# First layer of a two-layer trunk: gate values normalised on ScalarE, the gating half of the projection issued ahead of the convolution's LayerNorm, 13 convolution taps on ScalarE and GpSimd

## The chip, the cores and the metric

The kernel runs on one core of one Trainium2 chip. The time is device microseconds of one execution. The core's engines are named as in the profile: PE is the matmul engine (TensorE), with PEld for its weight loads; DVE is VectorE; ACT is ScalarE; POOL is GpSimd; SP issues the DMAs. Every engine works through its own instructions in a fixed order and waits on semaphores for the others.

## The reference

The trunk has two layers, each followed by an MLP, with 1024 tokens of width 1024, all float32. Only the first layer's mixer is touched by the change:

```python
def conv_gmlp_mixer(h, w_in, conv_w, conv_b, conv_ln_g, conv_ln_b,
                    sg_ln_g, sg_ln_b, sg_w, sg_b, w_out):
    z = h @ w_in
    a_val = z[..., :CONV_CH]                 # 512 channels each
    a_gate = z[..., CONV_CH:2 * CONV_CH]
    z_sg = z[..., 2 * CONV_CH:]
    a = a_val * jax.nn.sigmoid(a_gate)
    a = depthwise_conv(a, conv_w, width=31) + conv_b
    a = jax.nn.silu(layernorm(a, conv_ln_g, conv_ln_b))
    zs = jax.nn.gelu(z_sg, approximate=False)
    u = zs[..., :SG_CH]
    v = layernorm(zs[..., SG_CH:], sg_ln_g, sg_ln_b)
    v = v.reshape(B, S // 128, 128, SG_HEADS, SG_HEAD_DIM)
    v = jnp.einsum('gpq,bnqgc->bnpgc', sg_w, v) + sg_b.T[None, None, :, :, None]
    sg = u * v.reshape(B, S, SG_CH)
    return jnp.concatenate([a, sg], axis=-1) @ w_out

# per layer
shift, scale, gate = jnp.split(c_act @ mod_w + mod_b, 3, axis=-1)
h = rmsnorm(x, g) * (1 + scale) + shift
x = x + gate * mixer(h)
```

Here `depthwise_conv` stands for the reference's centred convolution along the tokens with one 31-tap filter per channel. The MLP that follows has its own `shift`, `scale` and `gate`.

## The kernel before, in words

Activations lie with channels on the 128 partitions and tokens along the free axis, in two column halves `c` of 512 tokens (`C = 512`, `NC = 2`). Every matmul product is made of three float32r matmuls (`mm3`, L128 to L132: high by high, high by low, low by high); so each weight stripe of 128x1024 is loaded as `raw`, cast to its high part `whi` on ACT (L112) and subtracted to its low part `wlo` on DVE (L113), in `prep`. Activations are split in the same way (`split`, L258: `zh` on ACT L259, `zl` on DVE L260).

The program is written in the order of the computation, but a planner of the framework (a timeline simulation at build time) sets each engine's fixed order from its own costs; `tc.high_priority` and manual dependencies bend it. The order on the chip is therefore that of the built program, not of the code.

The first layer goes through these stages:

1. RMSNorm of both column halves. `Norm.add` (L222) squares a block on ACT and adds it on DVE to a running sum; `Norm.fin` (L235) sums over partitions with one matmul against ones, and `rstd_of` makes the reciprocal root. The first 16 conditioning vectors are made by `mods(k)` beside this. Each is one `mod_unit` (L142): a DMA of 512 KB into `mraw`, and a DVE multiply with reduction (L147).
2. The projection of the convolution's values and gates; `glu` (L434) writes the padded inputs `ap` of four channel blocks of 128.
3. The gate values `vg`: projection, Gelu on ACT, statistics on DVE (L497, L498), and for each of 8 token chunks the normalisation as a DVE tensor_scalar (L509).
4. The projection of `u`, Gelu, and `gating(g)` for four heads: four small matmuls (L527), the eviction `tt` (L530) and the product (L534) on DVE, for each `g` and `c`. Then the split into `z[4..7]`.
5. The convolution (L579 to L603). For each of four blocks `i`, ACT makes the product of one tap (`pr`), POOL adds it to `a1` (L596): 11 taps in all, 10 of them with an add. DVE does the other `DVE_TAPS = 20` as a chain in PSUM, `ca` (L598 and L600), and adds `a1` at the end (L601).
6. LayerNorm over the 512 convolution channels: sums by PE with ones (L612), `y - mean` on DVE (L616), the squares on ACT, `rstd_of`; then, per block and column half, `y*rstd`, the sigmoid on ACT with the affine in its scale and bias, the affine itself on DVE (L633), the product on DVE (L635), and the split into `z[0..3]`.
7. The output projection in two halves (`project_half`): half 1 reads the gating's `z[4..7]`, half 0 the convolution's `z[0..3]`. Each is 16 outputs of 12 matmuls, each output followed by a residual update on DVE (`upd`, L283), which needs the conditioning's gate vectors: `queue_mod(0, [16])` queues these eight units, and `bg(n)` issues n queued units. 24 further units (`queue_mod(1, ...)`) are for the MLP. The planner orders each of these background units behind a chosen matmul (`newest`, L132) or behind POOL's last tap add (`conv_end`), and all of them share two buffers:

```python
            raw = cond.tile([P, D], F32, name="mraw", tag="mraw", bufs=2)
```

8. The MLP (first line in the trace: `mm3` with `b` or the first layer's `h`), unchanged, as is the whole second layer.

Half 1 of the projection stands in the code behind the LayerNorm, and so do all background units:

```python
        queue_mod(0, [16])
        bg(100)
        queue_mod(1, [8, 0], conv_end)
        queue_mod(1, [16])
        bg(18)
```

## Time and profile before

| what | us |
|---|---|
| median of 3 runs (lowest, highest) | 2315.51 (2313.82, 2316.77) |
| profiled execution: its own time | 2312.99 |
| profiled execution: span | 2311.2 |
| PE busy (share of the span) | 2188.4 (95%) |
| DVE busy | 1867.0 (81%) |
| ACT busy | 1180.8 (51%) |
| POOL busy | 238.5 (10%) |
| granted TensorE clock, mean | 0.982 |

The span runs from the first to the last instruction; the time has 1.8 us more around it. Busy times of different engines overlap, so only the waits of the engine that is nearly always busy, PE, add up to time. In the slices, one digit stands for 57.8 us, in tenths. In rows of instructions, the name left of the arrow is written, those right of it are read, and the bracket is the idle time ahead of it on its engine with what ended it.

### The profile page before, as it was taken

The numbers are of one execution on the slowest core, as the hardware profiler recorded it, in microseconds if no ns is written. First come the engines' busy times: TensorE is split into PE (matmuls) and PEld (weight loads), VectorE is DVE, ScalarE is ACT, GpSimd is POOL, SyncE is SP. The second block draws the span as 40 slices with busy tenths as digits, with TensorE's granted clock in tenths as the row PEclk, the third lists the DMA queues.
The fourth block names the chain that finished last, engine by engine and source line by source line (L and its number), as shares of the span: only waits on it lengthen the run. The fifth ranks groups of instructions, "written<-read, shape, count | busy, mean of one in ns | idle before, by whom it ended". The sixth has DMA issues, their size and how long they took to land. (4 is left out here: it accounts for less than half of the span.)

```text
span 2311.2 us, 27508 instructions
## 1 busy us (share of the span) xinstructions
PE 2188.4 (95%) x10144; PEld 1800.3 (78%) x10144; DVE 1867.0 (81%) x2582; ACT 1180.8 (51%) x1753; POOL 238.5 (10%) x126
## 2 busy tenths in 40 slices
PE   4997599999999999979999999999999999999997
PEld 3786387778888888858888888887778888888886
DVE  8899899997785976986878878876699659578497
ACT  4554246643534535455666666654366354353455
POOL 0484000000000000031111111111100000000002
PEclk9998799999999999989999999999999999999999
DMA  8221553838448267233445333361353461643712
GB/s 319 84 73 46 192 168 131 319 112 284 178 165 284 97 224 250 91 114 90 93 92 109 68 90 73 77 205 51 114 216 121 163 229 48 214 140 111 245 45 73
DMA packets 113863, 335.17 MB, mean 145 GB/s; under 512 B 20576, under 2 KB 23520, under 8 KB 112704
## 3 DMA queue, kind: packets, MB, share of 16 engines
q1 hardware_dynamic: 113728, 333.41, 44.6%
q8 instruction: 80, 1.31, 0.2%
q14 instruction: 55, 0.45, 0.1%
HBM read 279.79 MB, written 53.58 MB: 144 GB/s over the span
## 5 line engine op out<-in xcount | busy, mean ns | idle before, releaser
L131 PE MATMUL ps<-b,whi 128*128 128x512 f32 (+1 forms) x1808 | 701.4, 389 | 6.7 <-DVE b L260 6.7
L130 PE MATMUL ps<-b,whi 128*128 128x512 f32 (+1 forms) x1808 | 692.8, 390 | 5.1 <-ACT b L259 4.6
L132 PE MATMUL ps<-b,wlo 128*128 128x512 f32 (+1 forms) x1808 | 693.6, 388 | 1.9 <-DVE wlo L260 1.9
L259 ACT CAST whi<-raw 128x1024 fp32r<-128x1024 f32 (+1 forms) x225 | 236.5, 1051 | 356.1 <-PE ps L131 310.1
L131 PEld LDWEIGHTS ps<-b,whi 128*128 128x128 f32 x1808 | 340.7, 188 | 79.7 <-DVE b L260 9.5
L130 PEld LDWEIGHTS ps<-b,whi 128*128 128x128 f32 x1808 | 340.3, 188 | 77.0 <-ACT b L259 3.9
L132 PEld LDWEIGHTS ps<-b,wlo 128*128 128x128 f32 x1808 | 340.4, 188 | 72.1 <-DVE wlo L260 2.7
L260 DVE TENSOR_TENSOR wlo<-raw,whi 128x1024 fp32r<-128x1024 f32 x224 | 273.0, 1219 | 137.4 <-ACT whi L259 135.5
L130 PE MATMUL ps<-hh,whi 128*128 128x512 f32 x576 | 225.0, 403 | 40.7 <-ACT hh L254 23.5
L131 PE MATMUL ps<-hl,whi 128*128 128x512 f32 x576 | 229.4, 399 | 4.1 <-DVE hl L255 2.6
L132 PE MATMUL ps<-hh,wlo 128*128 128x512 f32 x576 | 227.9, 396 | 0.0
L113 POOL TENSOR_TENSOR wlo<-raw,whi 128x1024 fp32r<-128x1024 f32 x32 | 83.7, 2619 | 1188.3 <-ACT whi L112 1027.4
L967 ACT ACTIVATE L<-L,mn 128x1024 f32<-128x1024 f32 x128 | 147.1, 1150 | 90.3 <-DVE mn L965 89.0
L748 DVE SCALAR_TENSOR_TENSOR x<-ps,mod,x 128x512 f32<-128x512 f32 x220 | 159.3, 744 | 38.6 <-PE ps L132 38.3
L965 DVE CUSTOM_DVE_ANT_0 L<-S,B 128x1024 f32<-128x1024 f32 x128 | 155.9, 1223 | 37.1 <-PE pt L987 18.2
L130 PEld LDWEIGHTS ps<-hh,whi 128*128 128x128 f32 x576 | 109.7, 191 | 67.9 <-ACT hh L254 27.2
L259 ACT CAST b<-f 128x512 fp32r<-128x512 f32 x192 | 118.0, 618 | 76.5 <-PE ps L132 74.6
L260 DVE TENSOR_TENSOR b<-f,b 128x512 fp32r<-128x512 f32 x192 | 128.6, 683 | 10.0 <-ACT b L259 10.0
L131 PEld LDWEIGHTS ps<-hl,whi 128*128 128x128 f32 x576 | 110.5, 192 | 29.3 <-DVE hl L255 5.5
L132 PEld LDWEIGHTS ps<-hh,wlo 128*128 128x128 f32 x576 | 110.4, 192 | 24.1 <-issue 0.5
L147 DVE CUSTOM_DVE_ANT_0 mraw<-mraw,cact 128x1024 f32<-128x1024 f32 x96 | 116.1, 1217 | 6.2 <-DMA mraw<-in_modw 6.2
L737 ACT COPY f<-ps 128x512 f32<-128x512 f32 x96 | 56.3, 590 | 122.8 <-PE ps L132 122.6
(199 smaller groups left out, 3478.8 us busy)
## 6 DMA issues: line engine op xcount, KB each, us to landing
b<-tspl SPq DMA_DIRECT2D x168, 512.0 KB, 5.2
raw<-in_wm SPq DMA_DIRECT2D x128, 512.0 KB, 4.3
mraw<-in_modw SPq DMA_DIRECT2D x96, 512.0 KB, 4.6
tspl<-b SPq DMA_DIRECT2D x56, 512.0 KB, 4.2
raw<-in_wqkv SPq DMA_DIRECT2D x24, 512.0 KB, 4.7
raw<-in_wo SPq DMA_DIRECT2D x17, 512.0 KB, 3.5
x<-in_xT SPq DMA_DIRECT2D x32, 256.0 KB, 5.8
tsr<-tsp SPq DMA_DIRECT2D x8, 1024.0 KB, 7.7
```

What stands on the lines that cost most here:

```text
L113: (eng or dve).tensor_tensor(out=lo, in0=raw, in1=f32(hi), op=ALU.subtract)
L130: pe.matmul(ps, wh, ah, start=first, stop=False, skip_group_check=resumed)
L131: pe.matmul(ps, wh, al, start=False, stop=False, skip_group_check=resumed)
L132: newest[0] = pe.matmul(ps, wl, ah, start=False, stop=last, skip_group_check=resumed)
L147: i = dve.tensor_tensor_reduce(out=raw, in0=raw, in1=cact, op0=ALU.mult, op1=ALU.add, scale=1.0, scalar=0.0, accum_out=acc)
L259: act.copy(out=out_h, in_=src)
L260: (lo_eng or dve).tensor_tensor(out=out_l, in0=src, in1=f32(out_h), op=ALU.subtract)
L737: act.copy(out={"X1": c11, "Y1": c22, "X2": c12}[p], in_=ps)
L748: dve.scalar_tensor_tensor(out=x[m][c], in0=ps, scalar=gate(d, m), in1=x[m][c], op0=ALU.mult, op1=ALU.add)
L965: dve.tensor_tensor_reduce(out=L, in0=S, in1=win, op0=ALU.add, op1=ALU.min, scale=1.0, scalar=3e38, accum_out=mn)
L967: act.activation(out=L, in_=L, func=AF.Exp, bias=mn, scale=-1.0, accum_out=s[:, j:j + 1])
```

## The change

It is made of seven edits, all in the first layer:

- `Norm.add_pe` is new: for the second column half, each squared block goes straight into a PE matmul against ones (8 matmuls that accumulate in one bank), in place of seven DVE adds and one matmul.
- `vg` is normalised on ACT (Identity with a scale and a bias per chunk) and no longer on DVE. A small DVE instruction makes the bias.
- `queue_mod(0, [16])`, `bg(100)` and half 1 of the projection are issued ahead of the convolution's code.
- `DVE_TAPS` goes from 20 to 18. ACT and POOL do 13 taps, with 12 POOL adds per block in place of 10.
- `a1` starts with the convolution's bias in it. For blocks 1 and 2 the DVE chain starts from `a1`, and its last tap writes `a0`; blocks 0 and 3 start with a bare multiply and add `a1` at the end as before.
- The affine behind the LayerNorm moves from DVE to ACT.
- `bg(18)` is issued behind the making of `z[0..3]`.

```diff
--- before.py
+++ after.py
@@ -31,7 +31,7 @@
 SUB_EPS = 1e-5
 TAPS = 31
 PAD = TAPS // 2
-DVE_TAPS = 20
+DVE_TAPS = 18
 B_BUFS = 8
 
 V_MIXG, V_MLPG, V_FING = 0, 16, 32
@@ -218,6 +218,16 @@
 
         def __init__(self):
             self.s, self.n, self.rstd = {}, {}, {}
+
+        def add_pe(self, c, xt, first, last):
+
+            if first:
+                self.s[c] = bank()
+            sq = tmp.tile([P, C], F32, name="sq", tag="sq", bufs=2)
+            act.activation(out=sq, in_=xt, func=AF.Square)
+            pe.matmul(self.s[c], ones, sq, start=first, stop=last)
+            if last:
+                self.rstd[c] = rstd_of(self.s[c], D, eps_r)
 
         def add(self, c, xt, width=C):
             n = self.n[c] = self.n.get(c, 0) + 1
@@ -392,8 +402,7 @@
                 load_x(1)
             block(k, 0)
         for m in range(KT):
-            nrm.add(1, x[m][1])
-        nrm.fin(1)
+            nrm.add_pe(1, x[m][1], m == 0, m == KT - 1)
         for k in range(3):
             block(k, 1)
         for k in range(3, KT):
@@ -505,9 +514,9 @@
         dve.tensor_tensor(out=vt, in0=vr, in1=vr, op=ALU.mult)
         dve.tensor_tensor(out=vt, in0=vt, in1=vv, op=ALU.mult)
         dve.scalar_tensor_tensor(out=vr, in0=vt, scalar=1.5, in1=vr, op0=ALU.add, op1=ALU.mult)
+        dve.scalar_tensor_tensor(out=vt, in0=mv[:, :, 0], scalar=-1.0, in1=vr, op0=ALU.mult, op1=ALU.mult)
         for t in range(8):
-            dve.tensor_scalar(out=vg[t], in0=vg[t], scalar1=mv[:, t, 0:1], scalar2=vr[:, t:t + 1],
-                              op0=ALU.subtract, op1=ALU.mult)
+            act.activation(out=vg[t], in_=vg[t], func=AF.Identity, scale=vr[:, t:t + 1], bias=vt[:, t:t + 1])
 
 
         ps = bank()
@@ -579,6 +588,12 @@
                 if half == 0:
                     nrm.add(c, x[m][c])
 
+        queue_mod(0, [16])
+        bg(100)
+        for i in range(4):
+            for c in range(NC):
+                project_half(1, c, i)
+
 
         acc = []
         for i in range(4):
@@ -589,18 +604,23 @@
             def cw(w):
                 return vcol(V_CW + w * 4 + i)
 
-            act.activation(out=a1, in_=a[:, DVE_TAPS:DVE_TAPS + T], func=AF.Copy, scale=cw(DVE_TAPS))
+            act.activation(out=a1, in_=a[:, DVE_TAPS:DVE_TAPS + T], func=AF.Identity, scale=cw(DVE_TAPS),
+                           bias=vcol(V_CB + i))
             for w in range(DVE_TAPS + 1, TAPS):
                 pr = mp.tile([P, T], F32, name="pr", tag="pr", bufs=2)
                 act.activation(out=pr, in_=a[:, w:w + T], func=AF.Copy, scale=cw(w))
                 conv_end = pool.tensor_tensor(out=a1, in0=a1, in1=pr, op=ALU.add)
             ca = cvps.tile([P, T], F32, name="ca", tag="ca")
-            dve.tensor_scalar(out=ca, in0=a[:, 0:T], scalar1=cw(0), scalar2=vcol(V_CB + i), op0=ALU.mult, op1=ALU.add)
+            if i in (1, 2):
+                dve.scalar_tensor_tensor(out=ca, in0=a[:, 0:T], scalar=cw(0), in1=a1, op0=ALU.mult, op1=ALU.add)
+            else:
+                dve.tensor_scalar(out=ca, in0=a[:, 0:T], scalar1=cw(0), scalar2=None, op0=ALU.mult)
             for w in range(1, DVE_TAPS):
-                dve.scalar_tensor_tensor(out=ca, in0=a[:, w:w + T], scalar=cw(w), in1=ca, op0=ALU.mult, op1=ALU.add)
-            dve.tensor_tensor(out=a0, in0=ca, in1=a1, op=ALU.add)
+                dst = a0 if i in (1, 2) and w == DVE_TAPS - 1 else ca
+                dve.scalar_tensor_tensor(out=dst, in0=a[:, w:w + T], scalar=cw(w), in1=ca, op0=ALU.mult, op1=ALU.add)
+            if i not in (1, 2):
+                dve.tensor_tensor(out=a0, in0=ca, in1=a1, op=ALU.add)
             acc.append(a0)
-
 
 
         rs = []
@@ -618,11 +638,8 @@
                     act.activation(out=sq, in_=y, func=AF.Square)
                     last = pe.matmul(pvar, ones, sq, start=i == 0, stop=i == 3)
             rs.append(rstd_of(pvar, 512, eps_l, after=last if c == 0 else None))
-        queue_mod(0, [16])
-        bg(100)
         queue_mod(1, [8, 0], conv_end)
         queue_mod(1, [16])
-        bg(18)
         for c in range(NC):
             cs = slice(c * C, (c + 1) * C)
             for i in range(4):
@@ -630,14 +647,11 @@
                 dve.tensor_tensor(out=y, in0=y, in1=rs[c], op=ALU.mult)
                 sg = tmp.tile([P, C], F32, name="sg", tag="ht", bufs=3)
                 act.activation(out=sg, in_=y, func=AF.Sigmoid, scale=vcol(V_CLG + i), bias=vcol(V_CLB + i))
-                dve.tensor_scalar(out=y, in0=y, scalar1=vcol(V_CLG + i), scalar2=vcol(V_CLB + i),
-                                  op0=ALU.mult, op1=ALU.add)
+                act.activation(out=y, in_=y, func=AF.Identity, scale=vcol(V_CLG + i), bias=vcol(V_CLB + i))
                 dve.tensor_tensor(out=y, in0=y, in1=sg, op=ALU.mult)
                 z[i][c] = htile()
                 split(*z[i][c], y)
-        for i in range(4):
-            for c in range(NC):
-                project_half(1, c, i)
+        bg(18)
 
         h = [[None] * NC for _ in range(KT)]
         for c, seq in ((0, (0, 1, 2, 3)), (1, (3, 2, 1, 4))):
```

The order of DVE changes most. The first place is the start of the convolution's block 1. In these rows `ca` is the PSUM chain, `ap` the padded input, `vec` the filter taps, `a1` POOL's sum, `a0` the result of a block, `wlo` the low part of a weight, and `st6` the statistics of a chunk of `vg`. Before, on DVE:

```order
L113 TENSOR_TENSOR wlo_1022<-raw_1019,whi_1021 128x1024 [waits DMAHW5_49,Activation_49]
L600 SCALAR_TENSOR_TENSOR ca_1701<-ap_623,vec_72,ca_1701 128x1024 [waits DVE_49] x2
L601 TENSOR_TENSOR a0_1668<-ca_1701,a1_1669 128x1024 [waits DVE_49,Pool_49]
L113 TENSOR_TENSOR wlo_1076<-raw_1073,whi_1075 128x1024 [waits DMAHW6_49,Activation_49]
L598 TENSOR_SCALAR ca_1756<-ap_746,vec_72 128x1024 [waits DVE_49]
L497 BN_STATS st6_1051<-vg_1049 128x6 [waits Activation_49]
L497 BN_STATS st6_1056<-vg_1054 128x6 [waits Activation_49]
```

The change, on DVE at the same place:

```order
L622 TENSOR_TENSOR a0_1886<-ca_1925,a1_1887 128x1024 [waits DVE_49,Pool_49]
L443 TENSOR_TENSOR ap_854<-ps_805,sg_857 128x512 [waits PE_49,Activation_49]
...
L113 TENSOR_TENSOR wlo_1075<-raw_1072,whi_1074 128x1024 [waits DMAHW6_49,Activation_49]
L506 BN_STATS st6_1050<-vg_1048 128x6 [waits Activation_49]
L615 SCALAR_TENSOR_TENSOR ca_1984<-ap_622,vec_72,a1_1946 128x1024 [waits Pool_49]
L506 BN_STATS st6_1055<-vg_1053 128x6 [waits Activation_49]
...
L620 SCALAR_TENSOR_TENSOR ca_1984<-ap_622,vec_72,ca_1984 128x1024 [waits DVE_49]
```

Block 1 (the second `ca`) began with a tensor_scalar that waits for nothing but DVE itself; it now begins with an instruction that reads `a1` and waits for POOL.

The second place is the end of the gating, also on DVE. Before (`tt` is the gating's eviction, `u` its product), the last tap of block 2 and the taps of block 3 (`ca_1811`) stand ahead of the first `tt`:

```order
L600 SCALAR_TENSOR_TENSOR ca_1756<-ap_746,vec_72,ca_1756 128x1024 [waits DVE_49] x2
L601 TENSOR_TENSOR a0_1723<-ca_1756,a1_1724 128x1024 [waits DVE_49,Pool_49]
L598 TENSOR_SCALAR ca_1811<-ap_855,vec_72 128x1024 [waits DVE_49]
L600 SCALAR_TENSOR_TENSOR ca_1811<-ap_855,vec_72,ca_1811 128x1024 [waits DVE_49]
L113 TENSOR_TENSOR wlo_1364<-raw_1361,whi_1363 128x1024 [waits DMAHW5_49,PE_49,Activation_49]
L600 SCALAR_TENSOR_TENSOR ca_1811<-ap_855,vec_72,ca_1811 128x1024 [waits DVE_49] x7
L530 SCALAR_TENSOR_TENSOR tt_1426<-ps_1421,vec_72,sgb_604 128x512 [waits PE_49]
L113 TENSOR_TENSOR wlo_1472<-raw_1469,whi_1471 128x1024 [waits DMAHW6_49,Activation_49]
```

The change, on DVE from the last products of heads 0 to 2 on; `zl` is the low half of the gated `u`, `mraw` a background unit:

```order
L543 TENSOR_TENSOR u_1392<-u_1392,tt_1458 128x512 [waits DVE_49]
L543 TENSOR_TENSOR u_1419<-u_1419,tt_1466 128x512 [waits DVE_49]
L270 TENSOR_TENSOR zl_1554<-u_1392,zh_1553 128x512 [waits PE_49,Activation_49]
L147 ISA mraw_1613,mod_73<-mraw_1613,cact_92 128x1024
...
L615 SCALAR_TENSOR_TENSOR ca_2042<-ap_745,vec_72,a1_2004 128x1024 [waits Pool_49]
L620 SCALAR_TENSOR_TENSOR ca_2042<-ap_745,vec_72,ca_2042 128x1024 [waits DVE_49]
L147 ISA mraw_1619,mod_73<-mraw_1619,cact_92 128x1024 [waits DMAHW2_49]
L147 ISA mod_73 128x1
L539 SCALAR_TENSOR_TENSOR tt_1534<-ps_1529,vec_72,sgb_603 128x512 [waits PE_49]
```

Six of the gating's eight evictions now stand ahead of block 2's first tap (`ca_2042`), which waits for POOL. The residual updates of half 1 stand among the taps of blocks 2 and 3, on DVE:

```order
L620 SCALAR_TENSOR_TENSOR ca_2042<-ap_745,vec_72,ca_2042 128x1024 [waits DVE_49]
L157 TENSOR_TENSOR mod_73<-mod_73,vec_72 128x8 [waits DVE_49]
L620 SCALAR_TENSOR_TENSOR ca_2042<-ap_745,vec_72,ca_2042 128x1024 [waits DVE_49]
L293 SCALAR_TENSOR_TENSOR x0_0_1581<-ps_1644,mod_73,x0_0_1581 128x512 [waits DMAHW1_49,DVE_49,PE_49]
L293 SCALAR_TENSOR_TENSOR x1_0_1583<-ps_1658,mod_73,x1_0_1583 128x512 [waits DMAHW2_49,PE_49]
...
L620 SCALAR_TENSOR_TENSOR ca_2042<-ap_745,vec_72,ca_2042 128x1024 [waits DVE_49]
L113 TENSOR_TENSOR wlo_1703<-raw_1700,whi_1702 128x1024 [waits PE_49,Activation_49]
```

Before, all of them stood behind the LayerNorm's first part.

The third place is the end of the convolution, on DVE. Before (L616 is `y - mean` of the LayerNorm):

```order
L600 SCALAR_TENSOR_TENSOR ca_1811<-ap_855,vec_72,ca_1811 128x1024 [waits DVE_49]
L157 TENSOR_TENSOR mod_73<-mod_73,vec_72 128x8 [waits DVE_49]
L600 SCALAR_TENSOR_TENSOR ca_1811<-ap_855,vec_72,ca_1811 128x1024 [waits DVE_49] x2
L601 TENSOR_TENSOR a0_1778<-ca_1811,a1_1779 128x1024 [waits DVE_49,Pool_49]
L616 SCALAR_TENSOR_TENSOR a0_1613<-ps_1833,a0_1613 128x512 [waits PE_49]
L616 SCALAR_TENSOR_TENSOR a0_1668<-ps_1833,a0_1668 128x512
L616 SCALAR_TENSOR_TENSOR a0_1723<-ps_1833,a0_1723 128x512
L616 SCALAR_TENSOR_TENSOR a0_1778<-ps_1833,a0_1778 128x512 [waits DVE_49]
L147 ISA mraw_1921,mod_73<-mraw_1921,cact_92 128x1024 [waits DMAHW1_49]
```

The change:

```order
L620 SCALAR_TENSOR_TENSOR ca_2100<-ap_854,vec_72,ca_2100 128x1024 [waits DVE_49]
L113 TENSOR_TENSOR wlo_2309<-raw_2306,whi_2308 128x1024 [waits DMAHW3_49,Activation_49]
L620 SCALAR_TENSOR_TENSOR ca_2100<-ap_854,vec_72,ca_2100 128x1024 [waits DVE_49] x14
L147 ISA mraw_2255,mod_73<-mraw_2255,cact_92 128x1024 [waits DMAHW1_49]
...
L147 ISA mraw_2258,mod_73<-mraw_2258,cact_92 128x1024 [waits DMAHW2_49]
...
L622 TENSOR_TENSOR a0_2061<-ca_2100,a1_2062 128x1024 [waits DVE_49,Pool_49]
L147 ISA mraw_2261,mod_73<-mraw_2261,cact_92 128x1024 [waits DMAHW7_49,DVE_49]
...
L147 ISA mraw_2264,mod_73<-mraw_2264,cact_92 128x1024 [waits DMAHW0_49,DVE_49]
...
L636 SCALAR_TENSOR_TENSOR a0_1886<-ps_2120,a0_1886 128x512 [waits PE_49]
```

Two background units now stand between the last tap and the add of `a1` (`a0_2061`), and two behind that add, ahead of the LayerNorm; half 1's updates are no longer behind it.

## The prediction

> **What bounds the kernel now.** I read the page's slices first, then the windows of the first layer, then PE's timeline with its idle times, then VectorE's instructions by form. The four rows of slices show where TensorE (PE) is not full: PE is at 9 tenths nearly everywhere, except in slice 1 and in slices 4 and 5 (about 173 to 289 us), and there VectorE (DVE) stands at 9.
>
> ```profile
> PE 2188.4 (95%) x10144; PEld 1800.3 (78%) x10144; DVE 1867.0 (81%) x2582; ACT 1180.8 (51%) x1753; POOL 238.5 (10%) x126
> PE   4997599999999999979999999999999999999997
> DVE  8899899997785976986878878876699659578497
> POOL 0484000000000000031111111111100000000002
> ```
>
> The windows (columns: stretch, length, then busy us of PE, PEld, DVE, ACT and POOL, clock, DMA) give the size of the hole: from 83 to 208 us PE is full, from 208 to 286 it is busy for 36.3 of 78, then full again.
>
> ```profile
> 10.00:50.00 40.00, 19.56 (x51) 11.64 (x52) 38.82 (x79) 18.00 (x27) 0.00 (x0) 0.96 1.04 389
> 50.00:83.00 33.00, 33.00 (x147) 27.25 (x145) 24.82 (x47) 14.75 (x19) 0.00 (x0) 1.00 0.17 56
> 83.00:208.00 125.00, 124.98 (x542) 100.30 (x541) 121.95 (x110) 74.81 (x82) 91.91 (x36) 1.00 0.23 73
> 208.00:286.00 78.00, 36.33 (x140) 23.88 (x138) 70.50 (x84) 17.26 (x24) 12.36 (x5) 0.72 0.46 152
> 286.00:377.00 91.00, 91.00 (x395) 73.89 (x394) 84.85 (x134) 46.13 (x64) 0.00 (x0) 1.00 0.47 155
> ```
>
> PE's timeline (start, length, line, tiles, and in brackets the idle time before) names the two waits in it, both for DVE: 15.0 us for the gating, whose eviction stands behind convolution taps, and 23.3 us for the last tap's add.
>
> ```profile
> 207.87 1.72 PE L527 MATMUL ps<-sgw,vg 128*128 128x128 f32 x14
> 229.34 0.79 PE L130 MATMUL ps<-hh,whi 128*128 128x512 f32 x1 [15.02 <-DVE tt L530]
> 234.62 0.41 PE L130 MATMUL ps<-hh,whi 128*128 128x512 f32 x1
> 270.62 1.22 PE L612 MATMUL ps<-a,ones_r 128*128 128x512 f32 x1 [23.27 <-DVE a L601]
> 376.03 0.39 PE L130 MATMUL ps<-zh,whi 128*128 128x512 f32 x1
> 376.71 0.39 PE L130 MATMUL ps<-b,whi 128*128 128x512 f32 x1
> ```
>
> The last row is the first matmul of the MLP. Up to there I follow both kernels; behind it the code is the same. Three matmuls lie between the last two rows, so one costs 0.227 us, and one half of the projection (192 matmuls) 43.6 us.
>
> **The change, part by part.** The durations come from these rows (line, operation, shapes, count, then busy us and mean ns). Starts follow one another about 0.08 us sooner than the durations say: a lone tap of 1.28 costs 1.19 (244.61 to 245.80), chained taps 1.31 (14.44 us for 11).
>
> ```profile
> L600 DVE SCALAR_TENSOR_TENSOR ca<-ap,vec,ca 128x1024 f32<-128x1024 f32 x76 | 97.5, 1283 | 1.5
> L113 DVE TENSOR_TENSOR wlo<-raw,whi 128x1024 fp32r<-128x1024 f32 x22 | 35.5, 1614 | 0.6 <-ACT whi L112 0.6
> L147 DVE CUSTOM_DVE_ANT_0 mraw<-mraw,cact 128x1024 f32<-128x1024 f32 x24 | 29.1, 1219 | 6.2 <-DMA mraw<-in_modw 6.2
> L509 DVE TENSOR_SCALAR vg<-vg,mv,vr 128x512 f32<-128x512 f32 x8 | 16.3, 2108 | 0.0
> L283 DVE SCALAR_TENSOR_TENSOR x<-ps,mod,x 128x512 f32<-128x512 f32 x20 | 14.9, 751 | 0.0
> L530 DVE SCALAR_TENSOR_TENSOR tt<-ps,vec,sgb 128x512 f32<-128x512 f32 x8 | 5.9, 743 | 0.0
> L633 DVE TENSOR_SCALAR a<-a,vec 128x512 f32<-128x512 f32 x8 | 4.1, 546 | 0.0
> 86.48 14.53 DVE L600 SCALAR_TENSOR_TENSOR ca<-ap,vec,ca 128x1024 f32<-128x1024 f32 x11
> 100.92 0.68 DVE L434 TENSOR_TENSOR ap<-ps,sg 128x512 f32<-128x512 f32 x1
> 237.16 1.58 DVE L260 TENSOR_TENSOR zl<-u,zh 128x512 fp32r<-128x512 f32 x1
> 241.12 0.68 DVE L260 TENSOR_TENSOR zl<-u,zh 128x512 fp32r<-128x512 f32 x1
> 244.61 1.28 DVE L600 SCALAR_TENSOR_TENSOR ca<-ap,vec,ca 128x1024 f32<-128x1024 f32 x1
> 245.80 0.68 DVE L534 TENSOR_TENSOR u<-u,tt 128x512 f32<-128x512 f32 x1
> ```
>
> Start-up: seven adds of 0.6 us leave DVE and eight sums enter PE, which is idle for half of 10 to 50 us. But in the new order three more background units (1.15 us each) stand on DVE ahead of the second half's reciprocal root. That gives back 3.4 of 4.2 us, and PE is full from 50 us on anyway: I take 0, with bounds of -4 (all of the saving) and +2.
>
> 83 to 208 us: PE's order here is unchanged and it has no hole, so what DVE sheds is worth nothing unless DVE uses the time for later work. It does not. Blocks 1 and 2 of the convolution now start from GpSimd's sum, which has 12 adds of about 2.5 us (25.66 us for ten, below): block 0's from 87 to 118 us, block 1's from about 120 to 152. DVE's queue has the first tap of block 1 behind that wait, and the first tap of block 2 behind the whole gating. So between 112 and 152 us and again from 190 to 208 us DVE mostly waits; before, it had by 208 us done blocks 0, 1 and most of 2. Taking the gate values' normalisation off DVE (16.3 us) is hidden in the same way: on ACT it is done at about 195 us, and PE asks for it at 207.87. This cover is PE's work. Were PE sooner, it would be worth more.
>
> From 208.9 us (the gating's first four small matmuls) DVE has one dense run up to the last tap: 8 gating evictions at 0.66 (5.3); 8 products and 8 low halves at 0.60 (9.6); of these, eight lie beside GpSimd's adds, and the pair at 237.16 and 241.12 shows 1.58 against 0.68 there, of which I take 0.7 each (5.6); 6 weight splits at 1.13, the first beside GpSimd at 2.1 (7.8); 8 units at 1.15 (9.2); 16 residual updates at 0.66, new at this place (10.6); 18 taps of block 2 (21.5) and 18 of block 3 (23.5). The sum is 93.1, so the taps end at 302.0 us, or at 295.4 if GpSimd costs nothing and everything else fits. Before, they ended at 269.2. GpSimd ends block 3 at the same time: ACT can feed it only behind a weight cast that waits until PE is through three quarters of the moved half (about 269 us), and its third add waits behind the next cast, until PE is through all of it (281); nine adds of 2.5 then end near 305.
>
> [...] Lengthening by 0.9 us is what the row at 237.16 shows. [...]
>
> LayerNorm: before, the moved half of the projection covered it; now PE has nothing to do until its first output. The rows: a unit (L147) reuses one of two buffers, and its load comes back 3.72 us after the buffer's release (278.74 to 282.46), a cycle of 4.87 us.
>
> ```profile
> 86.93 25.66 POOL L596 TENSOR_TENSOR a<-a,pr 128x1024 f32<-128x1024 f32 x10 [85.60 <-ACT pr L595]
> 278.74 0.08 DVE L147 DVE_READ_ACCUMULATOR2_ANT mod<- 128x1 f32 x1
> 282.46 1.23 DVE L147 CUSTOM_DVE_ANT_0 mraw<-mraw,cact 128x1024 f32<-128x1024 f32 x1 [2.39 <-DMA mraw<-in_modw]
> 269.35 1.23 DVE L601 TENSOR_TENSOR a<-ca,a 128x1024 f32<-128x1024 f32 x1
> 308.70 0.62 ACT L259 CAST zh<-a 128x512 fp32r<-128x512 f32 x1 [1.89 <-DVE a L635]
> ```
>
> In the new order fifteen units stand on DVE between the last tap and the first product with the sigmoid. The fifteenth can start seven cycles after the first, 34.1 us; with its own 1.15, the product 0.6 and the cast 0.7 the first output stands 36.6 us behind the last tap: 338.6 us. (Before it took 38 us from the last add, 269.35 to 308.70, with the affine on DVE.) DVE's own work in this stretch adds up to 30.8 us, which is the lower bound if loads were never late. Moving the affine to ACT (8 x 0.45) is therefore hidden behind the loads.
>
> Then PE needs 43.6 us for the other half, 1.0 for the norm's sum, and 2.4 more since it starts after idling: after the 15 us wait, thirteen matmuls took 5.3 us (229.34 to 234.62) instead of 2.9. End: 385.6 against 376.71, that is 8.9 us later. PE's holes have been filled with the moved half, and a hole of about the same size has come up behind it. The profiled execution took 2313.0 us (span 2311.2), so 2321.9; the median of the runs is 2.5 above the profile: 2324.
>
> **The rivals.**
>
> No change: DVE's run is not lengthened by GpSimd (the products' mean was 0.68 before, also in a busy stretch). Then the taps end at 295.4, everything behind is 6.6 us sooner, and the time is 2318. Against it speak the rows at 237.16 and L113's mean of 1614. Faster loads could give at most 5.8 us more; together that would be 2312.
>
> Faster: PE reaches the gating sooner. The place is 10 to 50 us, where PE idles for 20.4 us; with the sum of squares on PE the second half's reciprocal root no longer queues for adds, and if its matmuls filled that idle time, all that hangs on PE's 207.87 would move with it, one for one. It decides from 8.9 + 4.6 = 13.5 us on; with 15 us the time is 2309. Against it: by DVE's order the reciprocal root comes no sooner than now, and DMA is full there (1.04, 389 GB/s).
>
> [...]
>
> **How the numbers follow.** Two thousandths, 4.6 us, is about what a measurement of this kernel can tell from no change. Chances: the forecast (+4.6 to +11) 0.55, no change 0.25, faster 0.12, much slower 0.08. The range holds the first two: 2312 (no lengthening, and prompt loads) to 2335 (11 us of the forecast, with up to 8 more for PE's stalls in the 83 to 208 us stretch, where a late sum of block 1 holds weight splits behind it). Faster 0.12, same 0.25, slower 0.63.
>
> **What would show it.** Right: DVE idle for 25 us or more between 112 and 152 us, waiting for GpSimd's sum; gating still at 207 to 209; PE free of the 15 and 23 us waits, but with one of 25 to 45 us in front of the first zh of the convolution half; last tap near 302; units of L147 waiting for their loads behind it; first MLP matmul near 386. Wrong: DVE working on block 1 before 145 us, a last tap before 290, the first output less than 30 us behind it, or PE at the gating before 200.

## The result and the profile after

The changed kernel takes 2340.35 us (median of 4 runs, 2336.32 to 2341.82) against 2314.98 for the kernel before (2313.82 to 2316.77). The ratio is 1.011, with a 95% interval of 1.0097 to 1.0124: 25 us slower, where the forecast was 9 us slower and the range ended at 2335. The direction was right, the size was not.

The profiled execution took 2339.32 us, its span is 2337.2, which is 26.0 more than before. The first matmul of the MLP, which starts at 376.71 us before, is at 402.22. So 25.5 of the 26.0 us arise ahead of that matmul, and only that stretch is looked at here.

The slices of the page, PE and DVE (58.4 us each now). The hole in PE has moved from slices 4 and 5 to slice 6 (about 292 to 351 us), with a smaller one in slice 5:

```profile
PE   4999839899999999979999999999989999999998
DVE  7747989998696895996888888786599759668497
```

The windows of the same stretches as before (busy us of PE, PEld, DVE, ACT and POOL; clock; DMA):

```profile
83.00:208.00 125.00, 125.00 (x543) 100.43 (x542) 78.52 (x83) 71.97 (x81) 70.52 (x27) 1.00 0.24 77
208.00:286.00 78.00, 65.12 (x304) 53.13 (x303) 68.25 (x77) 24.73 (x31) 28.23 (x12) 0.93 0.43 146
286.00:377.00 91.00, 45.22 (x141) 28.14 (x140) 81.70 (x109) 41.59 (x54) 27.73 (x11) 0.74 0.41 128
```

In the first row, DVE's busy time has fallen from 121.95 to 78.52 us while PE stays full: 43 us of DVE work have left a stretch in which PE needed none of them. In the second, PE has gained 28.8 us of work, most of the moved half. In the third it has lost 45.8, since that half no longer covers the LayerNorm.

PE's timeline (idle time in brackets), with the first MLP matmul as the last row:

```profile
50.10 2.07 PE L130 MATMUL ps<-hh,whi 128*128 128x512 f32 x4 [9.29 <-ACT hh L264]
212.98 5.52 PE L536 MATMUL ps<-sgw,vg 128*128 128x128 f32 x48
249.57 2.50 PE L130 MATMUL ps<-zh,whi 128*128 128x512 f32 x5 [9.20 <-ACT zh L269]
321.06 2.07 PE L632 MATMUL ps<-a,ones_r 128*128 128x512 f32 x2 [27.05 <-DVE a L622]
356.14 2.93 PE L130 MATMUL ps<-zh,whi 128*128 128x512 f32 x6 [13.66 <-ACT zh L269]
402.22 0.39 PE L130 MATMUL ps<-b,whi 128*128 128x512 f32 x1
```

The wait of 15 us is gone, as forecast. The one of 23 us is not: it is PE's wait for the last convolution add (L601 before, L622 now), ahead of the LayerNorm's last sums, and it now takes 27.1 us and ends 50 us later. New are 9.3 us at the start, 9.2 at the end of the gating, and 13.7 ahead of the first output of half 0. (The forecast was a single wait of 25 to 45 us there; it came as 27.1 and 13.7, on both sides of the LayerNorm's last sums.) The gating starts at 212.98 and not at 207.87.

DVE's timeline at the places that the prediction named:

```profile
160.85 1.28 DVE L615 SCALAR_TENSOR_TENSOR ca<-ap,vec,a 128x1024 f32<-128x1024 f32 x1
214.07 0.75 DVE L539 SCALAR_TENSOR_TENSOR tt<-ps,vec,sgb 128x512 f32<-128x512 f32 x1 [4.52 <-PE ps L536]
218.85 1.37 DVE L113 TENSOR_TENSOR wlo<-raw,whi 128x1024 fp32r<-128x1024 f32 x1 [4.03 <-ACT whi L112]
220.14 2.86 DVE L543 TENSOR_TENSOR u<-u,tt 128x512 f32<-128x512 f32 x1
224.91 6.54 DVE L543 TENSOR_TENSOR u<-u,tt 128x512 f32<-128x512 f32 x3
232.03 2.19 DVE L270 TENSOR_TENSOR zl<-u,zh 128x512 fp32r<-128x512 f32 x1
234.81 0.68 DVE L270 TENSOR_TENSOR zl<-u,zh 128x512 fp32r<-128x512 f32 x1
296.21 18.51 DVE L620 SCALAR_TENSOR_TENSOR ca<-ap,vec,ca 128x1024 f32<-128x1024 f32 x14
316.51 3.35 DVE L147 CUSTOM_DVE_ANT_0 mraw<-mraw,cact 128x1024 f32<-128x1024 f32 x1
319.79 1.21 DVE L622 TENSOR_TENSOR a<-ca,a 128x1024 f32<-128x1024 f32 x1
```

Block 1's first tap (L615) comes at 160.85, when GpSimd's sum is ready; between 125 and 160 us DVE has little but weight splits to do. The last taps end at 314.72 (296.21 plus 18.51), forecast 302.0. GpSimd's own rows show what stands beside them:

```profile
126.48 33.97 POOL L612 TENSOR_TENSOR a<-a,pr 128x1024 f32<-128x1024 f32 x12 [2.40 <-ACT a L607]
205.98 27.70 POOL L612 TENSOR_TENSOR a<-a,pr 128x1024 f32<-128x1024 f32 x10 [7.20 <-ACT pr L611]
295.19 23.59 POOL L612 TENSOR_TENSOR a<-a,pr 128x1024 f32<-128x1024 f32 x9 [4.34 <-ACT pr L611]
```

Block 1's sum ends at 160.45, block 2's at 233.68 and block 3's at 318.78 (start plus length). The product at 220.14 and the three from 224.91 start beside block 2's adds and take 2.86 us and, on average, 2.18; the low half at 234.81, just behind the adds, takes 0.68. The average hides how the delay comes about. Two pairs of single instructions show it, first a product beside an add, then a weight split ahead of one:

```profile
225.35 2.73 POOL L612 TENSOR_TENSOR a<-a,pr 128x1024 f32<-128x1024 f32 x1
225.74 2.89 DVE L543 TENSOR_TENSOR u<-u,tt 128x512 f32<-128x512 f32 x1
133.51 1.41 DVE L113 TENSOR_TENSOR wlo<-raw,whi 128x1024 fp32r<-128x1024 f32 x1 [7.57 <-ACT whi L112]
133.92 3.26 POOL L612 TENSOR_TENSOR a<-a,pr 128x1024 f32<-128x1024 f32 x1
```

The product ends 0.55 us after the add that was running when it started (228.08 and 228.63), and all four products beside adds do the same: the one at 224.91 met an add near its end and took 0.91, the others 2.86 to 2.89. The weight split met the end of an add and took 1.41 in place of 1.22; the next add came second and took 3.26 in place of 2.41. So in these two pairs the loss falls on whichever comes second, and it is about what is left of the first: 2.21 us for the product, which met an add with 2.34 left, and 0.85 for the add, which met a split with 1.00 left. Five of block 1's 12 adds, whose sum DVE waits for, are lengthened in this way, by some 4 us together.

### The profile page after: what moved, and what is told of

Its sections match the earlier page's. It is cut to its first block, busy times and chain, and to the rows that moved or that the text cites. A ratio compares the mean times of both kernels' runs of the same rounds, so it can differ in the third digit from the quotient of the medians.

```text
span 2337.2 us, 27536 instructions
## 1 busy us (share of the span) xinstructions
PE 2196.0 (94%) x10158; PEld 1801.6 (77%) x10158; DVE 1839.2 (79%) x2550; ACT 1197.2 (51%) x1774; POOL 260.4 (11%) x134
## 5 line engine op out<-in xcount | busy, mean ns | idle before, releaser
L612 POOL TENSOR_TENSOR a<-a,pr 128x1024 f32<-128x1024 f32 x48 | 126.5, 2635 | 191.0 <-ACT pr L611 102.9
L132 PEld LDWEIGHTS ps<-hh,wlo 128*128 128x128 f32 x576 | 109.5, 190 | 24.6 <-issue 1.3
L147 DVE CUSTOM_DVE_ANT_0 mraw<-mraw,cact 128x1024 f32<-128x1024 f32 x96 | 119.2, 1250 | 6.8 <-DMA mraw<-in_modw 6.7
```

The source lines that it names most:

```text
L132: newest[0] = pe.matmul(ps, wl, ah, start=False, stop=last, skip_group_check=resumed)
L147: i = dve.tensor_tensor_reduce(out=raw, in0=raw, in1=cact, op0=ALU.mult, op1=ALU.add, scale=1.0, scalar=0.0, accum_out=acc)
L612: conv_end = pool.tensor_tensor(out=a1, in0=a1, in1=pr, op=ALU.add)
```

## Experiments

All were made from the changed kernel. A diff below is against it, or shows what a run adds to an earlier one that its text names. A difference "to the changed kernel" is between medians; the kernel before, run with each group, had medians of 2313.60 to 2314.98, so some 1.5 us of any such difference can be the chip's. The changed kernel itself was run only with the first group, and its four runs spread over 5.5 us. The planner sets every order anew, so an undone edit can move more than its own instructions.

**The start from GpSimd's sum, undone.**

```diff
-            if i in (1, 2):
+            if False:
-                dst = a0 if i in (1, 2) and w == DVE_TAPS - 1 else ca
+                dst = ca
-            if i not in (1, 2):
+            if True:
                 dve.tensor_tensor(out=a0, in0=ca, in1=a1, op=ALU.add)
```

> The changed kernel with one edit undone: blocks 1 and 2 of the convolution start with a bare multiply again and add GpSimd's sum at the end; 18 taps on DVE, and everything else, stay as changed. Theory (the start from GpSimd's sum leaves DVE idle from 126 to 160 us and in front of the gating, and this is the largest part of the loss): DVE works on blocks 1 and 2 ahead of the gating, its dense run behind the gating loses some 35 taps (45 us), the first output of the convolution half comes before 315 us, and the time falls by 30 to 50 us, to 2290 to 2310, below the kernel before. Rival (background units and their loads pace what stands behind the last tap, in any order): the fall is below 15 us, time over 2325.

Measured: 2311.63 us (2309.0 to 2315.02), ratio to before 0.9989 (0.9979 to 0.9998). That is 28.7 us below the changed kernel: this one edit costs more than the whole change loses, and what is left of the change is worth about 2 us, hardly more than nothing. The rival falls. The theory's size was a little too high (30 to 50 us), and its first output, "before 315", was wrong. DVE has a last add (L622) at 259.95 and then no LayerNorm until 302.94:

```profile
259.95 1.21 DVE L622 TENSOR_TENSOR a<-ca,a 128x1024 f32<-128x1024 f32 x1
302.94 2.48 DVE L636 SCALAR_TENSOR_TENSOR a<-ps,a 128x512 f32<-128x512 f32 x4
```

PE is busy with the moved half from 257 to 302 us without a break and comes to the LayerNorm's first sums (L632) only at 295.95. It gives the first output's matmul at 329.88 and the MLP's at 377.50:

```profile
257.19 2.50 PE L130 MATMUL ps<-zh,whi 128*128 128x512 f32 x5 [0.32 <-ACT zh L269]
295.95 3.60 PE L632 MATMUL ps<-a,ones_r 128*128 128x512 f32 x8
329.88 2.93 PE L130 MATMUL ps<-zh,whi 128*128 128x512 f32 x6 [11.69 <-ACT zh L269]
```

**The moved half of the projection, undone.** `queue_mod(0, [16])`, `bg(100)` and the loop over `project_half(1, c, i)` go behind the LayerNorm's code again.

```diff
-        queue_mod(0, [16])
-        bg(100)
-        for i in range(4):
-            for c in range(NC):
-                project_half(1, c, i)
...
+        queue_mod(0, [16])
+        bg(100)
         queue_mod(1, [8, 0], conv_end)
...
         bg(18)
+        for i in range(4):
+            for c in range(NC):
+                project_half(1, c, i)
```

> The changed kernel with one edit undone: the gating half of the projection and its eight gate vectors stand behind the LayerNorm's code again. Theory (moving the half ahead only moves PE's idle time, since DVE sets the end; alone it is a small gain): the taps end some 10 us sooner, since 16 residual updates leave the dense run, but PE then has both halves, 91 us, behind the last tap; the first MLP matmul comes at 400 to 412 us and the time is 2338 to 2350. Rival (the moved half, with its updates on DVE, is what made the kernel slower): the time falls by 12 us or more, below 2328.

Measured: 2358.93 us (2356.76 to 2362.71), ratio 1.0192 (1.0177 to 1.0207), 18.6 above the changed kernel. The rival, that the moved half made the kernel slower, falls clearly; beside the other edits the move is a gain, and twice the most that I gave it. (Moved alone, in the kernel before, it was not tried.) The last tap ends some 7 us sooner (308.1), but PE waits 50 and 25 us for the convolution, has the LayerNorm's sums first, and begins the first half only at 329.31 us:

```profile
284.31 2.08 PE L626 MATMUL ps<-a,ones_r 128*128 128x512 f32 x2 [50.16 <-DVE a L614]
311.57 2.08 PE L626 MATMUL ps<-a,ones_r 128*128 128x512 f32 x2 [25.19 <-DVE a L616]
329.31 0.80 PE L130 MATMUL ps<-zh,whi 128*128 128x512 f32 x1
```

With 91 us for both halves, the first MLP matmul comes at 420.34.

**The sum of squares on PE, undone.**

```diff
-            nrm.add_pe(1, x[m][1], m == 0, m == KT - 1)
+            nrm.add(1, x[m][1])
+        nrm.fin(1)
```

> The changed kernel with one edit undone: the second half's squares are summed by DVE adds again. Theory (the loss is a sum of separate delays, and 5.1 us of it come from the start-up: PE reaches the gating at 212.98 us in place of 207.87, because PE's own order now holds the squares' sums between the blocks and then waits 9.3 us): the gating's first small matmul is back near 208 us, the wait of 9.3 us near 41 us is gone, and the time falls by 4 to 6 us to about 2335. Rival (the dense run on DVE is set by GpSimd's sum of block 2, so PE's earlier arrival is hidden): time unchanged, 2338 to 2342.

Measured: 2346.52 us (2346.28 to 2348.61), ratio 1.0139 (1.0123 to 1.0154), 6.2 above the changed kernel. Both expectations missed. The wait of 9.3 us at the start is gone and GpSimd's first add comes 4.7 us sooner (87.62 in place of 92.30), so the start-up's 5 us are real. They are lost again at 159 us. ACT's queue holds the products `pr` for GpSimd, each waiting for an add, and the Gelu of `vg` (L505), which must free PE's banks, stands behind the last of them and a table load. PE and ACT there:

```profile
159.15 0.79 PE L130 MATMUL ps<-whi,hh 128*128 128x512 f32 x1 [3.34 <-ACT vg L505]
```

```profile
155.11 1.15 ACT L612 ACTIVATE pr<-ap,vec 128x1024 f32<-128x1024 f32 x1 [1.33 <-POOL a L613]
157.21 1.28 ACT L505 ACT_TABLE_LOAD   x1
158.50 2.06 ACT L505 ACTIVATE vg<-ps 128x512 f32<-128x512 f32 x4
```

The granted clock is 0.91 from 160 to 185 us, behind that wait, and the gating starts at 214.44. In the changed kernel PE comes 5 us later and does not wait there: GpSimd's pace, through ACT's queue, was the cover of the late start-up. The first MLP matmul is 2.8 us later than in the changed kernel; the rest of the 6 us lies behind it, and its cause stays open.

**Twenty taps on DVE again.**

```diff
-DVE_TAPS = 18
+DVE_TAPS = 20
```

> The changed kernel with 20 taps on DVE and 11 on ACT and GpSimd again; blocks 1 and 2 still start from GpSimd's sum. Theory (DVE waits for the sums): block 1's sum is ready some 10 us sooner (two adds less in each of blocks 0 and 1), which DVE can use; against it stand two more taps of 1.2 us in blocks 2 and 3 each; net 3 to 10 us below the changed kernel, 2330 to 2337. Rival (the two taps moved to GpSimd relieve DVE): time 2343 or more.

Measured: 2351.30 us (2349.42 to 2354.95), ratio 1.0171 (1.0152 to 1.019), 11.0 above the changed kernel. The theory falls, and the time is the rival's. GpSimd's block 1 does end 9.8 us sooner (150.61) and its block 3 at 306.95, but DVE's last add is at 331.04, 11.3 later than in the changed kernel. How much of that is the taps' doing stays open: four more taps in blocks 2 and 3 take some 4.9 us, but between the first gating eviction and that add DVE also does 17 background units in place of 10, which the planner's new order put there, and loses less beside GpSimd: some 5 us (a product takes 2.85, two weight splits 3.18 and 2.24) in place of some 11 (8.2 at the gating, 2.9 in two units). PE also waits for DVE's residual updates, which stand behind taps and behind the gate vectors:

```profile
275.03 0.80 PE L130 MATMUL ps<-zh,whi 128*128 128x512 f32 x1 [14.31 <-DVE x L293]
```

**The gate values normalised on DVE again.**

```diff
-            act.activation(out=vg[t], in_=vg[t], func=AF.Identity, scale=vr[:, t:t + 1], bias=vt[:, t:t + 1])
+            dve.tensor_scalar(out=vg[t], in0=vg[t], scalar1=mv[:, t, 0:1], scalar2=vr[:, t:t + 1],
+                              op0=ALU.subtract, op1=ALU.mult)
```

> The changed kernel with one edit undone: the gate values are normalised on DVE again. Theory (this edit was hidden, since DVE idles from 200 to 214 us): 8 instructions of 0.55 to 2.1 us on DVE, 4 to 17 us; ACT can feed GpSimd's block 2 some 5 us sooner; gating at 213 to 218; time 2336 to 2345, no clear change. Rival (the normalisation on ACT, ahead of GpSimd's products there, is part of the loss): time below 2333.

Measured: 2339.20 us (2335.57 to 2341.37), ratio 1.0106 (1.0089 to 1.0122), no difference to the changed kernel that can be told. The time is as expected, the reason is not: in the changed kernel DVE idles 8.2 and 4.5 us ahead of the gating, which hides only part of the work. Beside GpSimd's adds the eight instructions take 20.4 us, PE waits 1.0 and 2.0 us for them, and the first gating eviction comes at 224.47, 10.4 later. DVE and POOL there:

```profile
197.59 20.37 DVE L519 TENSOR_SCALAR vg<-vg,mv,vr 128x512 f32<-128x512 f32 x8
192.56 30.91 POOL L613 TENSOR_TENSOR a<-a,pr 128x1024 f32<-128x1024 f32 x12 [33.43 <-ACT a L608]
```

What pays it back is GpSimd: ACT, rid of the normalisation, feeds it without a break, block 2's sum ends at 223.47 in place of 233.68, and the products behind it take 0.68 us. The last tap ends at 312.25, 2.5 sooner. So a later start by 10 us and an earlier sum by 10 us nearly cancel.

**GpSimd and DVE: the product with one input in PSUM.** The eviction `tt` of the gating writes back to its own bank.

```diff
-                tt = tmp.tile([P, C], F32, name="tt", tag="ht", bufs=3)
+                tt = pm
```

> The changed kernel; only the gating's eviction now writes back to its PSUM bank and not to SBUF, so that the product (L543) has one SBUF input in place of two. Theory (a DVE instruction that reads two SBUF tiles waits for GpSimd's add, one that reads one SBUF and one PSUM tile, like the taps, does not): the products beside GpSimd fall from a mean of about 2.2 us to below 1.0, the dense run ends 4 to 7 us sooner, time 2333 to 2337. Rival (any DVE instruction is lengthened there, or the time only moves to the next one): products stay over 1.5 us, or the time stays at 2338 to 2342.

Measured: 2334.78 us (2333.49 to 2336.47), ratio 1.009 (1.0075 to 1.0105), 5.6 below the changed kernel; since the intervals of the two ratios overlap, the size is uncertain, and the first MLP matmul comes 2.6 sooner (399.61). GpSimd adds block 2 from 205.49 to 232.58 in this run; the products beside it now take what they take alone:

```profile
219.69 0.68 DVE L543 TENSOR_TENSOR u<-u,ps 128x512 f32<-128x512 f32 x1
222.27 0.67 DVE L543 TENSOR_TENSOR u<-u,ps 128x512 f32<-128x512 f32 x1
228.68 1.64 DVE L270 TENSOR_TENSOR zl<-u,zh 128x512 fp32r<-128x512 f32 x1
```

The low half at 228.68, with both inputs in SBUF, still takes 1.64. On the products, the theory stands.

**All units early, with the start from GpSimd's sum kept.** `queue_mod(0, [16])` and `queue_mod(1, [8, 0])` are queued ahead of the gate values' projection, and `bg(4)` is called at each of its weight stripes; the old places are empty.

```diff
+        queue_mod(0, [16])
+        queue_mod(1, [8, 0])
...
                 wh, wl = wv.get(4 * c + j)
+                bg(4)
...
-        queue_mod(0, [16])
-        bg(100)
...
-        queue_mod(1, [8, 0], conv_end)
...
-        bg(18)
```

> The changed kernel with all 24 background units (the residual's gate vectors and the MLP's scale and shift) issued during the gate values' projection, where DVE idles. Theory (units pace the chain from the last tap to the first output: 41 us where DVE's own work there is about 18): the chain shrinks to 16 to 25 us, the taps end some 10 us sooner, though GpSimd's block 3 may then end last, near 316 us; time 2305 to 2322. Rival (the chain's length is the LayerNorm's own, passing between PE, DVE and ACT): the chain stays over 35 us and the time is over 2328.

Measured: 2347.28 us (2345.1 to 2349.36), ratio 1.014 (1.0125 to 1.0155), 6.9 above the changed kernel. Half of the theory holds: from the LayerNorm's first sum on the last block to the first output it is 24.6 us (333.87 to 358.46) in place of 35.1 (321.06 to 356.14), so units did lengthen that chain by 10. But the last add is 12.8 later (332.59), and the time went the wrong way. The gating starts at 223.59, because weight splits stand behind units and PE waits for them (2.6, 2.7 and 1.5 us), and GpSimd's block 3 begins and ends later:

```profile
154.97 0.50 PE L131 MATMUL ps<-wlo,hh 128*128 128x512 f32 x1 [2.59 <-DVE wlo L113]
```

```profile
303.49 29.07 POOL L614 TENSOR_TENSOR a<-a,pr 128x1024 f32<-128x1024 f32 x12 [38.26 <-ACT a L609]
```

**Units early, without that start.** The first run has the undone start and the early units together. The second has 16 units early (`queue_mod(0, [16])`, `queue_mod(1, [8])`, `bg(3)`) and the other 8 behind the making of `z`; beside the undone start, its edits are these:

```diff
+        queue_mod(0, [16])
+        queue_mod(1, [8])
...
+                bg(3)
...
-        queue_mod(0, [16])
-        bg(100)
...
-        queue_mod(1, [8, 0], conv_end)
+        queue_mod(1, [0])
         queue_mod(1, [16])
...
-        bg(18)
+        bg(9)
```

> The changed kernel with blocks 1 and 2 started from a bare multiply (as in the run without the gate) and all 24 background units issued in the gate values' projection. With the gate alone undone, the last tap's add ended at 261.1 us and the first subtraction of the LayerNorm came at 302.9, with units of L147 waiting for their loads between them. Theory (those units are what is late there): the LayerNorm follows the last add within 5 us, the first output comes 16 to 28 us behind that add; but 24 units ahead of the gating also hold weight splits, as in the run with early units alone (gating at 223.6), so the last add is near 285 and the time 2290 to 2306. Rival (the LayerNorm waits for PE, which is still in the moved half): no gain over the run without the gate, 2308 or more.

> As the run before, but only 16 units (gate vectors, MLP scale) go into the gate values' projection, and the 8 of the MLP's shift stand behind the making of the convolution half's outputs. Theory: gating near 214 us, last add of the convolution near 275, first output near 300 to 306, first MLP matmul near 350; time 2280 to 2295, below both kernels. Rival (PE is late at the gating because DVE's units hold weight splits): gating past 220 and time over 2300.

Measured: 2327.13 us (2326.95 to 2328.83), ratio 1.0058 (1.0043 to 1.0073), and 2323.21 us (2320.66 to 2325.34), ratio 1.0038 (1.0024 to 1.0051). Both are slower than without early units (2311.63), and both theories fall. With 24 early units the chain behind the last add is as short as expected (the first output comes at 335.81, 25.6 us behind it), but that add comes at 310.21 and not near 285. With 16 units early the gating starts at 222.30, past the 220 that the rival named, and the last add is at 305.41. Ahead of the gating units push taps behind it: without early units 66 of the 72 taps start before the first gating eviction, with 16 early units 54, with 24 only 47. Products again lie beside GpSimd, three of them in 7.38 us:

```profile
239.36 7.38 DVE L547 TENSOR_TENSOR u<-u,tt 128x512 f32<-128x512 f32 x3
```

These two runs can't tell what held back the LayerNorm in the run without the start from GpSimd's sum, because their own last adds come too late (310.21 and 305.41). The trace of that run tells it: its last add ends at 261.2, and PE comes to the LayerNorm's first sums at 295.95, since all but the last matmuls of the moved half stand ahead of them in PE's queue. It was PE, not the units.

**The moved half in two parts.** In addition to the undone start from GpSimd's sum, half of the moved half goes back behind the LayerNorm.

```diff
-        for i in range(4):
+        for i in range(2):
             for c in range(NC):
                 project_half(1, c, i)
...
+        for i in range(2, 4):
+            for c in range(NC):
+                project_half(1, c, i)
         bg(18)
```

> The changed kernel without the start from GpSimd's sum, and with the gating half of the projection cut in two: four of its eight weight stripes' outputs (i = 0, 1) stay ahead of the convolution, four (i = 2, 3) go behind the making of the convolution half's outputs. With the gate alone undone, PE ran the whole moved half from 257 to 302 us, with the LayerNorm's sums behind it, and then waited 15 us for the LayerNorm. Theory (the half ahead fills one hole of PE and a hole of what is left opens at the LayerNorm; two quarters fill both): the LayerNorm's sums come near 280 us, PE's waits between 280 and 335 us fall from 15 to under 5 us, time 2297 to 2305. Rival (DVE's work up to the first output sets the end, wherever PE's matmuls stand): time 2309 to 2314, as without the gate.

Measured: 2304.65 us (12 runs, 2301.96 to 2307.38), ratio to before 0.9964 (0.9953 to 0.9974): faster than the kernel before by 0.4% (three of whose 28 runs beside it took 2305 to 2306 us) and 7.0 us below the run with the whole half moved, within the expectation. The LayerNorm's sums start at 275.20 and PE's waits between 280 and 335 us are 1.43, 1.09 and 0.57:

```profile
280.92 1.13 PE L639 MATMUL ps<-sq,ones_r 128*128 128x512 f32 x2 [1.43 <-ACT sq L638]
289.27 1.13 PE L639 MATMUL ps<-sq,ones_r 128*128 128x512 f32 x2 [1.09 <-ACT sq L638]
333.13 0.50 PE L132 MATMUL ps<-zh,wlo 128*128 128x512 f32 x1 [0.57 <-DVE wlo L113]
```

**Two additions to it:** `tt` in PSUM as above, and then also the squares summed by DVE again, as above.

> As the run before, and the gating's eviction written back to PSUM, so that its products have one SBUF input. Theory: the products' wait for GpSimd, some 4 us there, goes; 1 to 5 us below the run before. Rival: hidden, equal to it within 1.5 us.

> As the run before, and the second half's squares summed by DVE again. Theory (the 5 us of the start-up are real, but were lost again where ACT's queue, which follows GpSimd's adds, delayed the gate values' Gelu): the start-up is 5 us sooner, PE waits 2 to 4 us for ACT near 160 us, and the gating and the end come 0 to 3 us sooner than in the run before. Rival (the start-up's gain is kept in full where DVE is not idle for GpSimd): 4 to 6 us sooner.

Measured: 2311.28 us (2309.25 to 2313.0), ratio 0.9992 (0.9982 to 1.0001), and 2311.35 us (2309.73 to 2315.16), ratio 0.9995 (0.9983 to 1.0008). The first is 6.6 us worse, which neither side expected. The products are short again, so PE has its last wait for the gating's outputs behind it 6 us sooner (250.59 in place of 256.47). It then stops for 10 us, because the residual updates (L293) wait for the last of the eight gate vectors, and that unit's load stands in SP's queue behind sixteen reloads of `x`. PE, DVE and SP of the first of the two:

```profile
274.89 0.79 PE L130 MATMUL ps<-zh,whi 128*128 128x512 f32 x1 [10.07 <-DVE x L293]
```

```profile
271.59 1.22 DVE L147 CUSTOM_DVE_ANT_0 mraw<-mraw,cact 128x1024 f32<-128x1024 f32 x1 [5.56 <-DMA mraw<-in_modw]
```

```profile
255.63 9.48 SPq L87 DMA_DIRECT2D x<-in_xT  x16
265.51 1.00 SPq L87 DMA_DIRECT2D mraw<-in_modw  x2
```

In the run without the addition that load is the last of four issued ahead of the reloads, the eighth unit starts at 265.82 in place of 271.59, and PE does not wait:

```profile
252.78 9.76 SPq L87 DMA_DIRECT2D mraw<-in_modw  x4
262.64 9.24 SPq L87 DMA_DIRECT2D x<-in_xT  x16
```

The second shows what the run with the squares on DVE showed alone: PE waits 4.72 us for the Gelu of `vg` at 161.11, the gating is at 215.90, and nothing of the start-up is kept. Its expectation (0 to 3 us sooner) holds at its lower end.

## Why the prediction was right and wrong, step by step

The first MLP matmul was forecast at 385.6 us and came at 402.22. The way was right, the size was not: three of the four terms were too small, one was a little too large, and together they make up the 16.6 us:

| step | forecast | measured | error |
|---|---|---|---|
| DVE's dense run begins (first gating eviction) | 208.9 | 214.07 | +5.2 |
| from there to the last tap | 93.1 | 100.65 (to 314.72) | +7.5 |
| last tap to the first output on PE | 36.6 | 41.4 (to 356.14) | +4.8 |
| half 0 on PE, up to the MLP | 47.0 | 46.1 (to 402.22) | -0.9 |

- **Start-up, the step that failed first.** I took 0, with bounds of -4 and +2, since PE is full from 50 us on. It is full from 50 us on in both kernels, but with less done: eight sums sit between its blocks and end at 40.8 us, the reciprocal root then stands among DVE's units and is done at 47.42 in place of 42.03, and PE waits 9.3 us, as the row at 50.10 shows. "PE is full" at a later time bounds nothing about work that was due before it. That the 5.1 us can't be had back by undoing the edit (2346.52) is another matter: there ACT's queue takes them.
- **The cover and the idle DVE: right.** The 43 us that left DVE in the 83 to 208 us stretch bought nothing, DVE idled for GpSimd's sum, and its dense run ended later than the taps did before. What I did not see is how much this one edit weighed. I told the result as one hole filled and another opened; with one edit undone at a time, the moved half is worth 18.6 us, the two taps 11 (in part by the planner's new order), the sum of squares on PE 6.2, and the start from GpSimd's sum costs 28.7. Each figure holds beside the other edits only: added up, they would make the change some 6 us faster, and it is 25 slower.
- **GpSimd's price, misread.** I took 0.7 us for each of eight operations, 5.6 in all, from the one row at 237.16, which is 0.9 us longer than the low half at 241.12, and gave a much slower kernel a chance of 0.08: by my estimate 14.4 us more, 2338, if each of the eight waits for a whole add of 2.5 us. Measured, four products and one low half take 11.59 us in place of 5 x 0.68, 8.2 more; the later ones come when GpSimd is done. What they pay is about what is left of the add that they meet, 2.21 us at most, and what my row paid was of the same kind. It started 1.03 us before the end of this add of the kernel before (238.19), and it too ended 0.55 us behind it (238.74):

```profile
235.43 2.76 POOL L596 TENSOR_TENSOR a<-a,pr 128x1024 f32<-128x1024 f32 x1 [17.03 <-ACT pr L595]
```

So it did not speak against a wait for a whole add: it met its add with 1.03 of 2.76 us left. Two runs show what an input in PSUM is worth to the product: beside adds it takes up to 2.89 us with both inputs in SBUF (the changed kernel) and 0.67 to 0.68 with one of them in PSUM (the run with `tt` in PSUM). That one SBUF input is not enough, L509 shows in the kernel before: it reads one SBUF tile and two scalars per partition and writes to SBUF, and it takes 2.62 us where it starts at 200.00 beside an add, 0.54 at 193.89 without; why, no run shows. The time landed near that 2338, but by luck, by other steps: contention brought 2.6 of the missing 16.6 us in the dense run, not 14.4.
- **A wait that I left out.** The weight split at 218.85 waits 4.03 us for ACT's cast, which stands behind products for GpSimd. I had counted the split, not what is queued ahead of its cast. With the 2.6 us of contention this makes 6.6 of the dense run's 7.5; the last 0.9 stays open.
- **The chain behind the last tap.** The pace by the units' loads was right in kind. It came 4.8 us longer: two units lie beside GpSimd's last adds and take 1.95 and 3.35 us in place of 1.22, 2.9 more, and the add at 319.79 stands behind the second, which ends only after GpSimd's last add (318.78). I had GpSimd end at 305. What made up the other 1.9 us stays open.
- **Right:** the wait of 15 us is gone, half 0 takes its 46 us, and moving the gate values' normalisation is worth nothing in time (2339.20 with it undone). The reason that I gave for the last, that it is hidden behind PE, is wrong: undone, it moves the gating's first eviction by 10.4 us, and GpSimd's earlier sum makes up for it.

Of the seven edits, two were not undone by themselves: the affine on ACT, and `bg(18)`. No run shows what the affine is worth. With `bg(18)` back in its old place the built program has the same order on every engine, so that edit does nothing.

## What to carry to other kernels

An accumulator that starts from another engine's sum is a wait at the head of the chain, where every instruction behind it in the queue waits too (this kernel lost 28.7 us by it); the same sum added at the end costs one instruction (1.21 us). Work moved into a hole should be cut to the hole: without that start, half of the moved projection in front and half behind filled two holes and beat both kernels (2304.65 us), where all of it in front left PE busy when the LayerNorm could have begun. And relief of a busy engine counts only from the place where a later engine waits for it (the 43 us taken off DVE between 83 and 208 us bought nothing): before counting it, find what the freed queue runs next and what that waits for.

## What was not expected of the hardware

- Beside GpSimd's adds, in the changed kernel, taps with one input in PSUM took 1.27 to 1.29 us throughout, while a product of two SBUF tiles went from 0.68 to up to 2.89, and a unit (L147) from 1.22 to 3.35. The delay is about what is left of the running add: products of 128x512 end 0.55 us behind it, units and weight splits of 128x1024 1.08 (the unit at 316.51 ends at 319.86, the add at 318.78). It works both ways: adds that come second, behind a weight split or a unit, take 3.2 to 3.35 us in place of 2.35 to 2.41. The number of SBUF inputs does not decide alone, since L509 with one such tile was held up too (2.62 us in place of 0.54, in the kernel before).
- An engine's in-order queue passed another engine's pace on to a third: GpSimd's adds do not feed PE there, yet in the two runs with the squares on DVE PE waited 3.34 and 4.72 us near 160 us for a Gelu that stood in ACT's queue behind products for GpSimd.
- A load can be late by its place in SP's queue: in the first run with an addition, sixteen reloads of `x` took 9.48 us to issue, and the last gate vector's load, issued behind them, held PE for 10.07.
